# Attention projections of a hybrid decoder block: q and k of four heads moved together, v first

## The chip, the cores and the metric

The kernel runs on one core of one Trainium2 chip. The metric is the time of one execution on the device, in microseconds (us); the time of a kernel is the median of its runs.

## The reference

One decoder layer on 1024 tokens of width 1024. The part that matters here is branch A, attention in three groups of eight heads of width 64, each group with its own window and dilation:

```python
h = rms_norm(x, norm_mix)
proj = h @ w_in                                  # 1024 x 1024 by 1024 x 10768
qkv_a, ... = split_columns(proj, IN_WIDTHS)      # 3 x 1536 columns: q, k, v
qkv_a = qkv_a.reshape(b, s, 3, 3, 8, 64)         # (q,k,v) x group x head x width
qa = rms_norm(qkv_a[:, :, 0], q_norm)            # over the 64 of a head
ka = rms_norm(qkv_a[:, :, 1], k_norm)
for gi, (win, dil) in enumerate(((128, 1), (512, 4), (2048, 16))):
    o_g, lse_g = dilated_window_attention(qa[:, :, gi], ka[:, :, gi], va[:, :, gi], win, dil)
o_a = sum(softmax(lse over the groups) * o_g)
...
```

Behind it stand a gated DeltaNet branch, gates, an output projection, a mixture of 16 experts and a last gated addition. The change does not touch them.

## The kernel before

All matmuls of the projections are made in three passes over split operands: each fp32 operand is written as a rounded part and a rest, and `mm3` (L36) issues rounded x rounded, rounded x rest and rest x rounded. `norm_h` (L128) normalises x and leaves its transpose split in `k.hh` and `k.hl` (eight blocks c of 128 channels by 1024 tokens). Weights come in pieces of 512 KB: `wraw` (L169) issues the transfer on SP's queue into one of two raw buffers, and `wsplit` (L177) makes the two parts, the rounded one on ScalarE (L182), the rest on VectorE (L183), in one of three pairs of buffers.

The attention stage (`attention`, L1310) has six units u of four heads: `hh, g = divmod(u, 3)` gives half and group. `attn_stream` (L355) projects one unit: first q, then k, then v, each in eight token tiles t of 128, each tile 24 matmuls (8 blocks, 3 passes) with the hidden state stationary and 256 weight columns moving, and yields once per tile: 24 pieces of 24 matmuls. ScalarE copies each result out of PSUM (L403) and, for q and k, squares it (L406); VectorE sums the squares per head (L407). After four tiles `norm` (L366) takes the inverse root (`rsqrt_ln`, L114: logarithm and exponential on ScalarE, small operations on VectorE), multiplies (L369) and queues two turns, each of which transposes four token tiles on PE (L374) into the one buffer of the PSUM pool `ps_t` and copies them to `qT` or `kT` on ScalarE with the gain (L378); the list `late` hands out one turn per piece. v of the groups 1 and 2 is regrouped through DRAM (`regroup`, L345). The weights of the next third are loaded at t = 5 (L417).

`attn_heads` (L425) is the softmax of a unit in ten steps: step i transposes the weights of token tile i-1 (`turn`, L465), multiplies those of tile i-2 with v (`value`, L475), and makes the scores of tile i (`score`, L447), which VectorE masks while it takes the maximum (L450, L452) and ScalarE exponentiates (L454). A tile sees 256 keys in group 0 (but for its first tile) and in every other tile of group 1, else 128.

The loop of `attention` (L1332) advances the softmax of unit u while it iterates over the projection of unit u+1, by the rule of L1343: step n comes with piece i when `10 * (i + 1) // 24` reaches it, so a step every 2 or 3 pieces. Beside unit 3 run `group_weights` and `combine_groups` (L508, L562), which combine the three groups of the first half; their scale-and-add is on VectorE (L582, L584), with broadcast transfers on SP's queue (L596). The last unit runs beside gate jobs (`channels`, L201, 512 moving columns), four yields per group, ten steps over 40 yields. Between unit 0's projection and the first softmax stand the decay tables (`dn_tables`, L223). A scheduler orders each engine's instructions from this program; it keeps near to the program's order.

Of the kernel before, what the change touches and what calls it, by code (L numbers as in the profile page):

```python
# [7 lines left out]
F32 = mybir.dt.float32  # L8
# [3 lines left out]
AF = mybir.ActivationFunctionType  # L12
ALU = mybir.AluOpType
AX = mybir.AxisListType
# [5 lines left out]
T = 8  # L20
C = 8
# [106 lines left out]
def norm_h(k):  # L128

    nc = k.nc  # L130
# [4 lines left out]
    v = k.I["norm_mix"]  # L135
    xs = []
    for t in range(T):
        if t % 2 == 0:
            xx = k.at.tile([128, 2, 1024], F32, name="x", tag="kT" if t < 4 else "vtok", bufs=2)
        x = xx[:, t % 2, :]  # L140
        for i in range(2 if t < 2 else 1):
            hs = slice(512 * i, 512 * i + 512) if t < 2 else slice(None)
            (nc.scalar if t < 2 and not i else nc.sync).dma_start(x[:, hs], k.I["x"][0, t * 128:t * 128 + 128, hs])
        if t == 0:
            nc.scalar.dma_start(g, bass.AP(tensor=v.tensor, offset=v.offset, ap=[[0, 128], [1, 1024]]))
        if t == 1:
            raw = attn_weights(k, 0, 0, 0, wraw)
        xs.append(x)
    for t in range(T):
        x = xs[t]  # L150
# [5 lines left out]
        if t == 0:  # L156
            with k.tc.issue_after(d.ins), k.tc.issue_after(k.last_exp.ins):
                ws = [wsplit(k, r) for r in raw]
# [64 lines left out]
def dn_tables(k):  # L223
# [9 lines left out]
    bc = k.at.tile([128, 1024], F32, name="bac", tag="qT", bufs=2)[0:32]  # L233
# [96 lines left out]
def attn_weights(k, g, hh, j, load=wload):  # L330
    w = k.I["w_in"][0].rearrange("(s c p) n -> s p c n", p=128, s=2)
    o = 1536 * j + 512 * g + 256 * hh
    return [load(k, [(slice(None), w[s][:, :, o:o + 256])], shape=(4, 256)) for s in range(2)]
# [21 lines left out]
def attn_stream(k, u, out, ws=None):  # L355
# [5 lines left out]
    ws = ws or attn_weights(k, g, hh, 0)  # L361
    late = []
# [3 lines left out]
    def norm(j, hf, raw, ss, dst):  # L366
        v = raw.rearrange("p t (h d) -> p (t h) d", d=64)
        rs = rsqrt_ln(k, at, ss[:, 4 * hf:4 * hf + 4, :].rearrange("p a b -> p (a b)"), 64.0)
        nc.vector.tensor_tensor(v, v, rs[:, :, None].to_broadcast([128, 16, 64]), op=ALU.mult)  # L369

        def turn(pr):
# [6 lines left out]
            nc.scalar.activation(turned_view(dst[:, pr, :], g, hf), src, AF.Copy, scale=k.gq if j == 0 else k.gk)  # L378
        late.extend([None, lambda: turn(0), lambda: turn(1)])

    for j in range(3):
        if j == 2:
            v = at.tile([128, T, 256], F32, name="vtok", bufs=2)
            out.append(v)
        if j == 2 and g == 0:
            rows = [v[:, t, :] for t in range(T)]
        elif j == 2:
            raw = [at.tile([128, 4, 256], F32, name="qraw", bufs=3) for _ in range(2)]
            rows = [raw[t // 4][:, t % 4, :] for t in range(T)]
        else:  # L390
            raw = [at.tile([128, 4, 256], F32, name="qraw", bufs=3) for _ in range(2)]
            rows = [raw[t // 4][:, t % 4, :] for t in range(T)]
            ss = at.tile([128, T, 4], F32, name="ss", bufs=2)
            dst = at.tile([128, 2, 1024], F32, name="qT" if j == 0 else "kT", bufs=2)
            out.append(dst)
        nxt = None
        for t in range(T):
            p = k.ps_mm.tile([128, 256], F32, name="mm", tag="mm")
            for c in range(C):
                hi, lo = ws[c // 4]  # L400
                s = slice(t * 128, t * 128 + 128)
                mm3(nc, p, k.hh[:, c, s], k.hl[:, c, s], hi[:, c % 4, :], lo[:, c % 4, :], c == 0, c == C - 1)
            nc.scalar.activation(rows[t], p, AF.Copy)  # L403
            if j < 2:
                sq = at.tile([128, 4, 64], F32, name="sqa", bufs=2)
                nc.scalar.activation(sq.rearrange("p a b -> p (a b)"), p, AF.Square)  # L406
                nc.vector.tensor_reduce(ss[:, t, :], sq, axis=AX.X, op=ALU.add)  # L407
            if late:
                f = late.pop(0)
                if f:  # L410
                    f()
            if j < 2 and t % 4 == 3:
                norm(j, t // 4, raw[t // 4], ss, dst)
            if j == 2 and g and t % 4 == 3:
                regroup(k, g, t // 4, raw[t // 4], v)
            if j < 2 and t == 5:
                nxt = attn_weights(k, g, hh, j + 1)  # L417
            yield
        ws = nxt
    for f in late:  # L420
        if f:
            f()
# [887 lines left out]
def attention(k):  # L1310
    tc, nc = k.tc, k.nc
    with ExitStack() as e:
# [6 lines left out]
        k.at = e.enter_context(tc.tile_pool(name="at", bufs=1, reuse_waits="tile"))  # L1319
        setup(k)  # L1320
# [11 lines left out]
        for u in range(6):  # L1332
            heads = attn_heads(k, u, *st)
# [6 lines left out]
            for i, _ in enumerate(attn_stream(k, u + 1, st) if u < 5 else more):  # L1340
# [541 lines left out]
```

## Time and profile before

| | |
|---|---|
| median of 3 runs | 2051.33 us (2045.94 to 2053.91) |
| the profiled execution, its own time | 2063.92 us |
| its span | 2062.2 us |
| PE busy | 1962.6 us, 95% |
| VectorE, ScalarE busy | 1161.1 us, 968.1 us |
| moved by DMA | 252.53 MB, mean 122 GB/s |

The profiled execution takes 12.6 us more than the median of the runs. The attention stage ends at about 592 us of the span. Matmuls are pipelined: the time from one start to the next is their cost, the durations overlap.

### The profile page before, as it was taken

How to read it: one execution, taken by the hardware profiler on the slowest of the kernel's cores; microseconds unless marked ns; L12 is line 12 of the kernel's file. 1: busy time of each engine (PE TensorE's matmuls, PEld its weight loads, DVE VectorE, ACT ScalarE, POOL GpSimd, SP SyncE). 2: the span in 40 equal slices, each digit the busy share in tenths (PEclk: the TensorE clock that was granted, in tenths of full speed). 3: DMA queues.
4: the chain of work that ended last, by engine and by line, in shares of the span. 5: the costliest groups of instructions: out<-in, count | busy, mean ns of one | idle time of the engine just before them, and what ended most of it. 6: DMA issues, size and time to landing. Idle time of an engine off the chain costs nothing.

```text
span 2062.2 us, 35105 instructions
## 1 busy us (share of the span) xinstructions
PE 1962.6 (95%) x13402; PEld 1672.1 (81%) x13402; DVE 1161.1 (56%) x2940; ACT 968.1 (47%) x2573; POOL 195.4 (9%) x196
## 2 busy tenths in 40 slices
PE   7999999999999989999999999979999889999998
PEld 7999999989987777777777777858978767777698
DVE  7253435473422678778877872355474645555655
ACT  6344445444443644565456452232433345555643
POOL 0000000000000001010000100000021244431100
PEclk9999999999999999999999999989999899999999
DMA  4102131242233222232222223585465377776742
GB/s 160 54 28 78 53 105 52 81 138 74 66 110 111 58 67 59 65 85 62 79 76 74 68 68 101 145 246 192 145 204 184 125 238 253 231 246 229 244 157 91
DMA packets 249353, 252.53 MB, mean 122 GB/s; under 512 B 62453, under 2 KB 207142, under 8 KB 248922
## 3 DMA queue, kind: packets, MB, share of 16 engines
q1 hardware_dynamic: 234280, 224.88, 35.8%
q0 software_dynamic: 11776, 24.18, 3.4%
q8 instruction: 107, 1.75, 0.3%
q10 hardware_dynamic: 3122, 1.16, 0.2%
q14 instruction: 68, 0.56, 0.1%
HBM read 202.34 MB, written 64.59 MB: 129 GB/s over the span
## 4 chain that ended last, share of the span: by engine, by line
PE 63%; DVE 14%; DMA 12%; issue 7%; ACT 2%; POOL 1%; SPq 1%; ACTq 0%; DVEq 0%; POOLq 0%
PE mm L37 13%; PE mm L38 13%; PE mm L39 12%; DMA M<-dA 4%; DVE prod L764 3%; DVE tu L766 3%; DMA wraw<-in_w_expert_down_dram 2%; PE gp L37 2%; DVE acc L636 2%; PE gp L39 2%; PE gp L38 1%; PE sc L447 1%; PE pv L475 1%; PE gu L37 1%; PE gu L38 1%
## 5 line engine op out<-in xcount | busy, mean ns | idle before, releaser
L183 DVE TENSOR_TENSOR wlo<-wraw,whi 128x1024 fp32r<-128x1024 f32 x228 | 274.9, 1223 | 213.2 <-ACT whi L182 211.3
L37 PE MATMUL mm<-whi,hTh 128*128 128x256 f32 x1152 | 336.1, 292 | 5.9 <-ACT sqa L406 3.5
L37 PE MATMUL mm<-hTh,whi 128*128 128x512 f32 x768 | 327.0, 426 | 14.7 <-ACT th L962 10.3
L38 PE MATMUL mm<-wlo,hTh 128*128 128x256 f32 x1152 | 327.8, 285 | 0.0
L39 PE MATMUL mm<-whi,hTl 128*128 128x256 f32 x1152 | 327.7, 284 | 0.0
L182 ACT ACTIVATE whi<-wraw 128x1024 fp32r<-128x1024 f32 x228 | 236.0, 1057 | 194.2 <-PE mm L38 113.9
L39 PE MATMUL mm<-hTh,wlo 128*128 128x512 f32 x768 | 304.8, 397 | 0.0
L38 PE MATMUL mm<-hTl,whi 128*128 128x512 f32 x768 | 303.8, 396 | 0.0
L37 PEld LDWEIGHTS mm<-whi,hTh 128*128 128x128 f32 x1152 | 221.8, 193 | 18.0 <-issue 7.3
L38 PEld LDWEIGHTS mm<-wlo,hTh 128*128 128x128 f32 x1152 | 222.1, 193 | 0.8 <-DVE wlo L183 0.7
L39 PEld LDWEIGHTS mm<-whi,hTl 128*128 128x128 f32 x1152 | 221.8, 193 | 0.2 <-DVE rsqx L119 0.2
L37 PEld LDWEIGHTS mm<-hTh,whi 128*128 128x128 f32 x768 | 146.3, 191 | 40.8 <-ACT th L962 10.7
L39 PEld LDWEIGHTS mm<-hTh,wlo 128*128 128x128 f32 x768 | 145.2, 189 | 32.9
L38 PEld LDWEIGHTS mm<-hTl,whi 128*128 128x128 f32 x768 | 146.4, 191 | 22.4
L454 ACT ACTIVATE sm<-sm,nm 128x128 f32<-128x128 f32 (+1 forms) x192 | 84.3, 440 | 87.5 <-DVE nm L452 87.0
L403 ACT ACTIVATE qraw<-mm 128x256 f32<-128x256 f32 x128 | 48.4, 378 | 148.2 <-PE mm L39 148.0
L407 DVE TENSOR_REDUCE ss<-sqa 128x4 f32<-128x256 f32 x96 | 40.1, 418 | 133.0 <-ACT sqa L406 132.9
L636 DVE SCALAR_TENSOR_TENSOR acc<-xp,cols,acc 128x512 f32<-128x512 f32 x144 | 107.7, 748 | 8.1 <-ACT acc L634 5.1
L466 DVE COPY pT<-pt 128x256 f32<-128x256 f32 (+1 forms) x96 | 49.4, 540 | 105.0 <-PE pt L465 105.0
L764 DVE TENSOR_TENSOR prod<-tu,M 128x2 f32<-128x2 f32 (+30 forms) x248 | 83.7, 337 | 6.2
L1520 PE MATMUL gr<-wraw,hr 128*64 128x256 f32 x512 | 67.0, 381 | 9.7 <-ACT hr L1511 9.6
L37 PE MATMUL mm<-whi,mh 128*128 128x256 f32 x256 | 73.6, 289 | 0.1
(402 smaller groups left out, 4077.5 us busy)
## 6 DMA issues: line engine op xcount, KB each, us to landing
wraw<-in_w_in_dram SPq DMA_DIRECT2D x84, 512.0 KB
wraw<-in_w_expert_down_dram SPq DMA_DIRECT2D x30, 512.0 KB
wraw<-in_w_expert_gate_dram SPq DMA_DIRECT2D x60, 256.0 KB
wraw<-in_w_expert_up_dram SPq DMA_DIRECT2D x60, 256.0 KB
gT<-th SPq DMA_DIRECT2D x32, 256.0 KB
wraw<-in_w_branch_b_dram SPq DMA_DIRECT2D x16, 512.0 KB
gate<-gT SPq DMA_DIRECT2D x32, 256.0 KB
wraw<-in_w_out_dram SPq DMA_DIRECT2D x16, 512.0 KB
```

Source lines behind the costliest of these rows:

```text
L37: nc.tensor.matmul(out, lh, rh, start=start, stop=False)
L38: nc.tensor.matmul(out, lh, rl, start=False, stop=False)
L39: nc.tensor.matmul(out, ll, rh, start=False, stop=stop)
L182: nc.scalar.activation(hi, raw, AF.Copy)
L183: nc.vector.tensor_tensor(lo, raw, r32(hi), op=ALU.subtract)
L403: nc.scalar.activation(rows[t], p, AF.Copy)
L454: nc.scalar.activation(x.sm[:, h, :nk], x.sm[:, h, :nk], AF.Exp, bias=nm[:, h:h + 1], accum_out=ml[:, x.t, h, 1:2])
L466: nc.vector.tensor_copy(x.pT[:, 2 * pr:2 * pr + 2, :nk], pt[:, :, :nk])
L636: nc.vector.scalar_tensor_tensor(acc, xp[:, i:i + 512], k.conv(i, b), acc, op0=ALU.mult, op1=ALU.add)
L764: nc.vector.tensor_tensor(pr[:, :j, :n], tu[:, :j, :n], M[:, None, :n, r].to_broadcast([128, j, n]), op=ALU.mult)
L766: nc.vector.tensor_reduce(tu[:, :j, r], pr[:, :j, :n], axis=AX.X, op=ALU.add)
L1520: k.nc.tensor.matmul(self.p[64 * f:64 * f + 64], self.t[:, c, :], w[:, f], start=c == 0, stop=c == 7)
```

## The change

v is projected first, in eight tiles of 256 columns. q and k follow together, in eight tiles of 512 columns: a weight piece now holds two blocks c with 256 columns of q beside 256 of k (`attn_raw`, two transfers per piece), and there are four such pieces and two for v. `attn_next` takes the six pieces of every unit in one sequence: it splits the next raw piece and starts the transfer of the one after the following; a fourth pair of split buffers (`k.wx`) serves three pieces of every two units. The eight-tile q-k half yields twice per tile, after 12 and after 24 matmuls, so a unit still has 24 pieces. The normalisation works on q and k of four token tiles at once (32 head rows per token, 2048 elements). The turns of the first half of the tokens come in pairs in the middle of tiles 6 and 7, those of the second half (`pre`) in tiles 1 and 2 of the next unit's v. `qT` and `kT` have one buffer each and not two. The softmax steps start at piece 3 and end at piece 18: `(10 * (i - 2) + 16) // 17`.

```diff
-def attn_weights(k, g, hh, j, load=wload):
...
+def attn_raw(k, u, i):
+    hh, g = divmod(u, 3)
+    o = 512 * g + 256 * hh
+    if i < 2:
+        w = k.I["w_in"][0].rearrange("(s c p) n -> s p c n", p=128, s=2)
+        return wraw(k, [(slice(None), w[i][:, :, o + 3072:o + 3328])], shape=(4, 256))
+    w = k.I["w_in"][0].rearrange("(s c p) n -> s p c n", p=128, s=4)
+    return wraw(k, [((slice(None), slice(None), slice(256 * j, 256 * j + 256)),
+                     w[i - 2][:, :, o + 1536 * j:o + 1536 * j + 256]) for j in range(2)], shape=(2, 512))
+def attn_next(k):
+    u, i = divmod(k.an, 6)
+    own = k.wpool, k.wbufs
+    if (u % 2, i) in ((0, 1), (0, 5), (1, 3)):
+        k.wpool, k.wbufs = k.wx, (0, 1)
+    w = wsplit(k, k.ar.pop(0))
+    k.wpool, k.wbufs = own
+    k.an += 1
+    if k.an + 1 < 36:
+        k.ar.append(attn_raw(k, *divmod(k.an + 1, 6)))
+    return w
...
 def attn_stream(...):
-        late.extend([None, lambda: turn(0), lambda: turn(1)])
-    for j in range(3):
...
+        return [lambda pr=pr: turn(pr) for pr in (0, 2, 1, 3)]
+    v = at.tile([128, T, 256], F32, name="vtok", bufs=2)
+    for t in range(T):
...
+        nc.scalar.activation(raw[:, t % 4, :] if g else v[:, t, :], p, AF.Copy)
+        if t in (1, 2):
+            for f in pre[2 * t - 2:2 * t]:
+                f()
...
+        if t in (2, 4):
+            qk.append(attn_next(k))
+        if t == 7:
+            qk += [attn_next(k), attn_next(k)]
+        yield
...
+    for t in range(T):
...
+        if t == 6:
+            dst += [at.tile([128, 2, 1024], F32, name=n) for n in ("qT", "kT")]
+        p = k.ps_mm.tile([128, 512], F32, name="mm", tag="mm")
+        for c in range(C):
+            hi, lo = qk[c // 2]
+            mm3(nc, p, k.hh[:, c, s], k.hl[:, c, s], hi[:, c % 2, :], lo[:, c % 2, :], c == 0, c == C - 1)
+            if c == 3:
+                if t == 7 and u < 5:
+                    nxt.append(attn_next(k))
+                for f in late[:2] if t > 5 else ():
+                    f()
+                late = late[2:] if t > 5 else late
+                yield
...
+        if t == 7 and u < 5:
+            nxt.append(attn_next(k))
+        yield
...
 def attention(k):
-                while n < 10 * (i + 1) // (24 if u < 5 else 40):
+                while n < ((10 * (i - 2) + 16) // 17 if u < 5 else 10 * (i - 1) // 38):
```

How the order moves, at two places (the numbers are those of buffers). ScalarE beside the second unit's projection, from the exponentials (`sm,ml<-sm,nm`) of the first unit's tile 3 to those of its tile 4. Before:

```order
L454 ACTIVATE sm_1776,ml_1411<-sm_1776,nm_1777 128x256 x4
L403 ACTIVATE qraw_1682<-mm_1791 128x256
L406 ACTIVATE sqa_1817<-mm_1791 128x256
L378 ACTIVATE qT_1323<-qkT_1820,gq_391 128x4x128
L403 ACTIVATE qraw_1682<-mm_1826 128x256
L406 ACTIVATE sqa_1852<-mm_1826 128x256
L478 ACTIVATE ot_1664<-pv_1878 128x2x128
L120 ACTIVATE rsqy_1856<-rsqx_1855 128x16
L121 ACTIVATE rsqy_1856<-rsqy_1856 128x16
L454 ACTIVATE sm_1891,ml_1411<-sm_1891,nm_1892 128x256 x4
```

Now:

```order
L485 ACTIVATE sm_1443,ml_1194<-sm_1443,nm_1444 128x256 x4
L444 ACTIVATE qraw_1402<-mm_1404 128x512
L446 ACTIVATE sqa_1471<-mm_1404 128x512
L509 ACTIVATE ot_1344<-pv_1487 128x2x128
L485 ACTIVATE sm_1500,ml_1194<-sm_1500,nm_1501 128x256 x4
```

Before, the results of two projection tiles (`qraw` and `sqa` from two `mm`) stood between the two steps; now one stands there, of which half the matmuls lie ahead of the first step.

VectorE at the end of a half of four projection tiles, from the last sum of squares (`ss<-sqa`) to the product (`qraw<-qraw,rsqy`). Before:

```order
L407 TENSOR_REDUCE ss_1322<-sqa_1456 128x4
L119 TENSOR_SCALAR rsqx_1459<-ss_1322 128x16
L122 TENSOR_TENSOR rsqz_1461<-rsqy_1460 128x16
L123 SCALAR_TENSOR_TENSOR rsqz_1461<-rsqz_1461,rsqx_1459 128x16
L124 SCALAR_TENSOR_TENSOR rsqy_1460<-rsqz_1461,rsqy_1460 128x16
L369 TENSOR_TENSOR qraw_1320<-qraw_1320,rsqy_1460 128x1024
```

Now, at the end of the second unit's projection:

```order
L447 TENSOR_REDUCE ss_1736<-sqa_1918 128x8
L119 TENSOR_SCALAR rsqx_1921<-ss_1736 128x32
L183 TENSOR_TENSOR wlo_2044<-wraw_1890,whi_2043 128x1024
L122 TENSOR_TENSOR rsqz_1923<-rsqy_1922 128x32
L183 TENSOR_TENSOR wlo_2124<-wraw_1935,whi_2123 128x1024
L123 SCALAR_TENSOR_TENSOR rsqz_1923<-rsqz_1923,rsqx_1921 128x32
L124 SCALAR_TENSOR_TENSOR rsqy_1922<-rsqz_1923,rsqy_1922 128x32
L389 TENSOR_TENSOR qraw_1735<-qraw_1735,rsqy_1922 128x2048
```

Two weight splits (`wlo`) of the next unit's q and k now stand inside the normalisation, and the product is twice as wide.

On PE the order of the change has 12 matmuls of 512 columns between the softmax steps of pieces 8 and 9 and between those of pieces 13 and 14, and 24 of 256 columns between those of pieces 3 and 4; before, no two steps of the units 0 to 4 were closer than 48 of 256 columns. The first of the four turns of a unit's second half stands behind 61 matmuls of the next unit's v, the others follow after 7 matmuls each; in tiles 6 and 7 of q and k 4 and 6 matmuls of 512 columns separate the turns of a pair. Before, at least 24 matmuls stood between two turns.

## Rows read from the trace of the kernel before

**Rows 1.** The page: part 1 (busy time of each engine, its share of the span, instructions) and the first line of part 4 (the chain that ended last, share of the span by engine).

```profile
PE 1962.6 (95%) x13402; PEld 1672.1 (81%) x13402; DVE 1161.1 (56%) x2940; ACT 968.1 (47%) x2573; POOL 195.4 (9%) x196
...
PE 63%; DVE 14%; DMA 12%; issue 7%; ACT 2%; POOL 1%; SPq 1%; ACTq 0%; DVEq 0%; POOLq 0%
```

**Rows 2.** Busy time of each engine in three stretches of the attention stage (stretch and its length in us; busy us of PE, its weight loads, VectorE, ScalarE and GpSimd, with instruction counts; granted clock as a share of full speed; DMA share; GB/s).

```profile
110.00:390.00 280.00, 279.84 (x2453) 264.65 (x2452) 117.95 (x408) 128.95 (x409) 2.31 (x3) 1.00 0.22 64
390.00:440.00 50.00, 48.37 (x419) 44.91 (x417) 35.85 (x98) 21.92 (x73) 0.00 (x0) 1.00 0.52 149
440.00:592.00 152.00, 150.03 (x1258) 139.63 (x1259) 60.39 (x192) 67.08 (x205) 2.05 (x3) 0.98 0.29 83
```

**Rows 3.** Who waited for whom between 110 and 592 us (engine, tile and line that waited, what ended the wait: us in total, times, longest).

```profile
ACT qraw L403 <- PE mm L39: 128.3, 72, 4.5
...
PE mm L37 <- ACT sqa L406: 3.5, 1, 3.5
```

**Rows 4.** Timeline of PE in the middle of a projection group (start in us, duration, line, operation, output<-inputs, shapes). The start of one to the start of the next is what an instruction costs; durations overlap.

```profile
435.74 0.28 PE L37 MATMUL mm<-whi,hTh 128*128 128x256 f32 x1
...
437.78 0.28 PE L39 MATMUL mm<-whi,hTl 128*128 128x256 f32 x1
```

**Rows 5.** Timeline of PE in three stretches with 512 moving columns: gate jobs (the transposed hidden state moves; 21 matmuls from the first row to the second), an expert (the weights move; 17 matmuls) and the output projection (the weights are stationary; 12 matmuls).

```profile
594.44 0.39 PE L37 MATMUL mm<-hTh,whi 128*128 128x512 f32 x1
...
598.98 0.39 PE L39 MATMUL mm<-hTh,wlo 128*128 128x512 f32 x1
...
1662.86 0.39 PE L38 MATMUL gu<-wlo,hgh 128*128 128x512 f32 x1
...
1666.52 0.40 PE L39 MATMUL gu<-whi,hgl 128*128 128x512 f32 x1
...
1560.42 0.39 PE L37 MATMUL mm<-oah,whi 128*128 128x512 f32 x1
...
1562.99 0.40 PE L39 MATMUL mm<-oah,wlo 128*128 128x512 f32 x1
```

**Rows 6.** Timeline of one softmax step with 256 keys: the scores on PE, the first of four masks and the negated maximum on VectorE, then the exponentials of head 0, 2 and 3 on ScalarE; the row behind the last begins where that exponential's sum has been read.

```profile
142.80 1.13 PE L447 MATMUL sc<-kT,qT 64*128 64x256 f32 x8
...
143.96 0.42 DVE L450 CUSTOM_DVE_ANT_0 sm<-sc,m 128x256 f32<-128x256 f32 x1 [0.96 <-PE sc L447]
...
145.46 0.17 DVE L452 TENSOR_SCALAR nm<-ml 128x4 f32<-128x4 f32 x1
...
145.67 0.51 ACT L454 ACTIVATE sm<-sm,nm 128x256 f32<-128x256 f32 x1 [2.37 <-DVE nm L452]
...
146.67 0.49 ACT L454 ACTIVATE sm<-sm,nm 128x256 f32<-128x256 f32 x1
...
147.16 0.49 ACT L454 ACTIVATE sm<-sm,nm 128x256 f32<-128x256 f32 x1
...
147.65 0.36 ACT L403 ACTIVATE qraw<-mm 128x256 f32<-128x256 f32 x1
```

**Rows 7.** Timeline of PE where the matmul stream is broken: four transposes of q or k, then eight of the weights, then the scores, then the first two matmuls of the next group.

```profile
521.92 0.60 PE L374 MATMUL qkT<-ident,qraw 128*128 128x128 f32 x4
522.36 0.60 PE L465 MATMUL pt<-ident,sm 128*128 128x128 f32 x4
...
523.91 1.13 PE L447 MATMUL sc<-kT,qT 64*128 64x256 f32 x8
524.98 0.38 PE L37 MATMUL mm<-whi,hTh 128*128 128x256 f32 x1
525.20 0.28 PE L38 MATMUL mm<-wlo,hTh 128*128 128x256 f32 x1
```

**Rows 8.** Timeline of one softmax step with 128 keys: the scores, the next matmul on PE, the last exponential and the reading of its sum.

```profile
330.80 0.71 PE L447 MATMUL sc<-kT,qT 64*128 64x128 f32 x8
...
331.45 0.39 PE L37 MATMUL mm<-whi,hTh 128*128 128x256 f32 x1
...
333.89 0.39 ACT L454 ACTIVATE sm<-sm,nm 128x128 f32<-128x128 f32 x1
...
334.19 0.19 ACT L454 ACTIVATION_READ_ACCUMULATOR sm<-sm,nm 128x1 f32 x1
```

**Rows 9.** Timeline of a softmax step that VectorE delayed: the scores, a weight split and a normalising product that stand between the masks, and the last exponential with the copy behind it.

```profile
133.45 1.14 PE L447 MATMUL sc<-kT,qT 64*128 64x256 f32 x8
...
134.59 1.22 DVE L183 TENSOR_TENSOR wlo<-wraw,whi 128x1024 fp32r<-128x1024 f32 x1
...
136.59 1.22 DVE L369 TENSOR_TENSOR qraw<-qraw,rsqy 128x1024 f32<-128x1024 f32 x1
...
140.23 0.49 ACT L454 ACTIVATE sm<-sm,nm 128x256 f32<-128x256 f32 x1
...
140.72 0.36 ACT L403 ACTIVATE qraw<-mm 128x256 f32<-128x256 f32 x1
```

**Rows 10.** Groups of instructions between 110 and 592 us (line, engine, operation, names, shapes, count | busy us, mean ns of one | idle before them, and what ended it).

```profile
L183 DVE TENSOR_TENSOR wlo<-wraw,whi 128x1024 fp32r<-128x1024 f32 x30 | 36.7, 1225 | 43.0 <-ACT whi L182 43.0
...
L407 DVE TENSOR_REDUCE ss<-sqa 128x4 f32<-128x256 f32 x79 | 33.1, 419 | 117.5 <-ACT sqa L406 117.3
...
L182 ACT ACTIVATE whi<-wraw 128x1024 fp32r<-128x1024 f32 x30 | 31.6, 1054 | 8.4 <-PE mm L39 8.4
...
L369 DVE TENSOR_TENSOR qraw<-qraw,rsqy 128x1024 f32<-128x1024 f32 x20 | 24.5, 1223 | 0.3
...
L378 ACT ACTIVATE qT<-qkT,gq 128x512 f32<-128x512 f32 x20 | 13.6, 682 | 0.0
```

**Rows 11.** Timeline of VectorE from a mean square (L119) to the product with its inverse root (L369).

```profile
434.53 0.17 DVE L119 TENSOR_SCALAR rsqx<-ss 128x16 f32<-128x16 f32 x1
...
435.98 1.23 DVE L369 TENSOR_TENSOR qraw<-qraw,rsqy 128x1024 f32<-128x1024 f32 x1
```

**Rows 12.** Timeline of VectorE in the unit that combines the groups: a scale that waited for its broadcast (in brackets the idle time before it and what ended it).

```profile
431.79 1.17 DVE L582 TENSOR_TENSOR fb<-fb,og 128x512 f32<-128x512 f32 x1 [2.40 <-DMA fb<-fT]
```

More of the change, by code (lines that the diff above doesn't have):

```diff
@@ L146, in norm_h @@
         if t == 1:
-            raw = attn_weights(k, 0, 0, 0, wraw)
+            k.an, k.ar = 0, [attn_raw(k, 0, i) for i in range(2)]
         xs.append(x)
@@ L157, in norm_h @@
             with k.tc.issue_after(d.ins), k.tc.issue_after(k.last_exp.ins):
-                ws = [wsplit(k, r) for r in raw]
+                ws = [attn_next(k) for _ in range(2)]
         for j in range(2):
@@ new lines, in attn_stream @@
+    dst = []
+    late = []
+    nxt = []
+    for t in range(T):
+        if t % 4 == 0:
+            raw = at.tile([128, 4, 512], F32, name="qraw", bufs=2)
+            ss = at.tile([128, 4, 8], F32, name="ss", bufs=2)
+        if t == 6:
+            dst += [at.tile([128, 2, 1024], F32, name=n) for n in ("qT", "kT")]
+        p = k.ps_mm.tile([128, 512], F32, name="mm", tag="mm")
+        s = slice(t * 128, t * 128 + 128)
+        for c in range(C):
+            hi, lo = qk[c // 2]
[4 more added lines that the diff above has]
+                for f in late[:2] if t > 5 else ():
+                    f()
+                late = late[2:] if t > 5 else late
+                yield
+        nc.scalar.activation(raw[:, t % 4, :], p, AF.Copy)
+        sq = at.tile([128, 8, 64], F32, name="sqa", bufs=2)
+        nc.scalar.activation(sq.rearrange("p a b -> p (a b)"), p, AF.Square)
+        nc.vector.tensor_reduce(ss[:, t % 4, :], sq, axis=AX.X, op=ALU.add)
+        if t % 4 == 3:
+            late += norm(t // 4, raw, ss, dst)
+        if t == 7 and u < 5:
+            nxt.append(attn_next(k))
+        yield
@@ L425, in attn_heads @@
+    out += [*dst, v, nxt, late]
 def attn_heads(k, u, qT, kT, v):
@@ L1339, in attention @@
             first = chain(group_weights(k, 0), combine_groups(k, 0)) if u == 3 else None
-            for i, _ in enumerate(attn_stream(k, u + 1, st) if u < 5 else more):
+            for i, _ in enumerate(attn_stream(k, u + 1, st, ws, pre) if u < 5 else more):
+                if u == 5 and i == 1:
+                    for f in pre:
+                        f()
                 if first:
                     next(first, None)
-                while n < 10 * (i + 1) // (24 if u < 5 else 40):
+                while n < ((10 * (i - 2) + 16) // 17 if u < 5 else 10 * (i - 1) // 38):
                     next(heads, None)
```

74 lines of the change are left out of this document (21 added, 53 removed).

## The prediction

> **What bounds the kernel now.** I read the page first: TensorE is busy for 95% of the span and the chain that ended last lies on PE for 63% of it, VectorE and ScalarE come to about half [rows 1]. That is an average over stages, so I read the stretches of the attention stage, the only part that the diff touches. From 110 to 390 us PE is busy for 279.8 of 280 us, at the full granted clock (1.00, the 2.4 GHz level), while VectorE and ScalarE have more than half of their time free [rows 2]. The waits of 110 to 592 us say the same: ScalarE waits 128.3 us for projection matmuls, and PE waits for anything only once, 3.5 us, for a ScalarE square [rows 3]. So in this stage the time is the sum of PE's instructions. A change gains what it takes out of that sum, and loses every wait it opens, since no slack on PE absorbs one.
>
> **What a projection matmul costs.** Moving 256 columns, 17 steps from 435.74 to 437.78 us make 120 ns each [rows 4]. Moving 512, 20 steps of the gate jobs make 4.54 us, 227 ns; 16 of the experts, where the weights move as they will here, make 3.66 us, 229 ns; 11 of the output projection make 2.57 us, 234 ns [rows 5]. So 512 columns cost less than 2 x 120 = 240 ns: the difference of 107 ns is the extra 256 columns, and some 13 ns is paid per instruction, whatever its width.
>
> The Trainium skill, "TensorE: Matmul & The Clock Gate", section "Back-to-back issue gap", gives N/2.4 + 2.5 ns for a warm matmul. By it 256 columns cost 109 and 512 cost 216 ns, and merging two would give 2.5 ns instead of some 12. The rows disagree with it for both widths, so I take the rows.
>
> **The change, part by part.**
>
> *Merged matmuls.* Per head unit, q and k took 384 matmuls of 256 columns and now take 192 of 512; six units make 1152 merges. Each gives 240 - 227 = 13 ns at best and 240 - 234 = 6 ns at worst. I take 228, nearest to the rows where the weights move and to those right behind the attention stage: 12 ns x 1152 = **-13.8 us**, between -7.4 and -15.0. It is all on the path.
>
> *Short gaps between score and transpose.* Ten steps of the softmax of the unit before are woven into 24 pieces. They now start at piece 3 and end at piece 18, so three gaps per unit hold one piece and not two: one of 24 matmuls of 256 columns (2.88 us), two of 12 of 512 (2.74 us). Before, the gap was 5.76 us, and PE did not wait for it. With 256 keys the scores hold PE for 1.07 us [rows 7], and the last exponential ends 147.65 - 142.80 = 4.85 us after they start [rows 6]. PE arrives at 1.07 + 2.74 = 3.81 and needs the last head after six transposes of 0.11 us [rows 7], at 4.47: 0.4 us of wait. With 128 keys PE arrives at 0.65 + 2.74 = 3.39 and the last exponential is done at 334.28 - 330.80 = 3.48 [rows 8], before its transposes come up at 3.7: none. Of 15 short gaps six have 256 keys, two of them in the unit that also combines the groups (below). Four x 0.4 = **+1.6 us**. These are the chains when VectorE is free. A late one, held by a weight split and a normalising product, ended 140.72 - 133.45 = 7.27 us after the scores started [rows 9], so the upper end is 2.4 us more in each of 15 gaps, some 36 us. I take the free chain, because in the new order the products of q and k stand behind the last score and the splits are done about when the scores begin.
>
> *Normalising q and k together.* The product now covers 2048 elements: two of 1.22 [rows 10], 2.45 us. That of the second half of the tokens is followed on PE by the transposes, which stand 61 matmuls into the next unit's v: cover 61 x 0.12 = 7.3 us. In that time come the copy and square of the last group (two reads of 512 columns, 0.68 each [rows 10]), the reduction (twice 0.42 less its fixed part, about 0.7 [rows 10]), the 1.45 us from mean square to product [rows 11], two weight splits that the order puts in between (1.22 each [rows 10]) and the product: 1.4 + 0.7 + 1.45 + 2.45 + 2.45 = 8.4 us if nothing overlaps. ScalarE's half of a split does overlap the logarithm and exponential, so I take 8.0: PE waits 0.7 us at each of four unit boundaries, **+2.8 us** (0 to 6). At the first boundary the decay tables stand in between, and at the last the gate jobs do: **+1 us** for the two.
>
> *Turns in pairs.* The transposed q and k go through one PSUM buffer, and the second of a pair now follows after 7 matmuls of 256 columns: 0.44 + 0.84 = 1.28 us after the first begins. The first takes 0.60 on PE [rows 7] and 0.68 on ScalarE [rows 10], with a handover: 0.1 us, three times at four boundaries, **+1.2 us**. The pairs inside the q-k groups have 0.91 us or more and wait for nothing worth counting.
>
> *Breaks in the matmul stream.* Of 16 breaks per unit there were two where a turn and a softmax step shared one; now there are 18. The second matmul after a break comes 0.22 and not 0.12 us after the first [rows 7]: 2 x 5 x 0.1 = **+1 us**.
>
> *The unit that combines the groups* (390 to 440 us). VectorE runs its scale-and-add beside the softmax; one of its waits for a broadcast took 2.40 us [rows 12], and the one wait of PE in the stage, 3.5 us [rows 3], lies here. The new order spreads the softmax differently, so that wait can go. But its two short gaps cost 0.4 and, where a scale stands ahead of the masks, some 1.2, and a late broadcast up to 2.4 more. I take **0**, from -2 to +4.
>
> *Costed at nothing.* The copies, squares and sums of 512 columns are half as many; ScalarE and VectorE had slack, which hid them. Weight bytes are the same; each q-k piece is two transfers instead of one, hidden because a piece is fetched about a piece before its split, and the fourth split buffer lets both of the next unit's v pieces be split before q-k ends. If that cover went, v's first matmuls would wait for a split of 1.05 + 1.22 us [rows 10]. One buffer for qT and kT is written six pieces behind the last score that reads it.
>
> **Sum.** -13.8 + 1.6 + 2.8 + 1 + 1.2 + 1 + 0 = -6.2 us. Of the profiled execution's 2063.9 us this leaves 2057.7. The median of the runs shown is 12.6 us lower than that execution; the saving is the same there: 2051.3 - 6.2 = **2045 us**. A measurement of this kernel tells about 0.5% (10.3 us) from no change.
>
> **The rivals.**
>
> *The waits stay hidden.* For it: PE arrives late by less than 1 us in every wait priced above, and one more overlap closes each. Against it: no slack on PE. Then 12 to 15 us remain: 2037 to 2039 us, faster by more than the bound. Chance 0.30.
>
> *The short gaps run late* (slower). Place: the transposes of the three early steps per unit, behind the exponentials. If each is held as in rows 9, six gaps cost 0.4 + 2.4 and nine 5.9 - 3.7 = 2.2: 36.6 us, with the 6 us of the other terms and -13.8 some +29: 2080 us. It eats the gain from (13.8 - 6) / 15 = 0.5 us per gap, and reaches the bound on the slower side from 1.2 us. For it: chains of that length stand in the trace. Against it: what delayed them there has been moved away from the scores. Chance 0.11 for slower than the bound.
>
> *The saving is not per instruction.* If merging gave only 2.5 ns, 1152 merges would give 2.9 us, and with 7.6 us of waits the time would be 2056 us, within the bound. Against it: 227 ns at 512 columns [rows 5]. This is the page's rule named above; by it and by no row the gain vanishes. Chance 0.06.
>
> That the program would not do what the diff says is ruled out: the order of PE shows the matmuls of 512 columns and the gaps as counted.
>
> **How the numbers follow.** The forecast, saving kept and 4 to 14 us of waits, has 0.53; about 0.06 of it lies beyond the bound on the faster side. Faster 0.30 + 0.06 = 0.36; same 0.47 + 0.06 = 0.53; slower 0.11. The range reaches from the whole of the largest saving (2051 - 15, less 1 for the spread of a median) to the smallest with the waits as priced and the combining unit late (2051 - 7.4 + 7.6 + 4, and some 5 for late gaps): 2035 to 2060.
>
> **What would show it.** On the page: 384 rather than 1152 matmuls of 256 columns on each of the three lines, and 227 to 229 ns between those of 512. In the waits of the attention stage: transposes of the weights waiting for exponentials, 0.4 us each; transposes of q and k waiting for the product, under 1 us, four times. The stage's end moves from 592 to about 586 us, and the stages behind it keep their length. Wrong would be: a spacing near 234 (the saving is halved), waits of a microsecond or more in most short gaps (slower), or PE waiting for split weights at the start of v.

## The result, and the profile after

The changed kernel took **2065.05 us** (median of 6 runs, 2060.3 to 2068.4) beside 2052.03 for the kernel before (6 runs, 2045.9 to 2058.0): ratio 1.0059, 95% interval [1.0035, 1.0082], some 12 us slower where 6 us faster was forecast, and just outside the range of 2035 to 2060.

The profiled executions do not show this at first sight: after has a span of 2058.7 us, before one of 2062.2. The profiled execution of before was slower than every timed run of its kernel, that of after about as fast as the fastest of its own. So whole spans must not be compared here, and the stages must be read one by one. The last transposes of the second heads' group weights, which close the attention stage (its last unit runs beside the gate jobs, hence later than the 592 us of the prediction), move from 664.2 to 674.0 us: **the changed stage is 9.8 us longer**. The code behind it is the same, and what it takes differs between two executions by more than that.

The page of after, part 1 and the first line of part 4 (answers to [rows 1]):

```profile
PE 1963.8 (95%) x12250; PEld 1606.8 (78%) x12250; DVE 1154.3 (56%) x2832; ACT 962.0 (47%) x2453; POOL 194.5 (9%) x196
...
PE 48%; DVE 13%; DMA 11%; issue 4%; ACT 3%; SPq 1%; POOL 1%; DVEq 0%; ACTq 0%; POOLq 0%
```

The 1152 instructions less are there (13402 to 12250), and PE's busy time is no shorter. The same three stretches as [rows 2], and two of 12 us:

```profile
110.00:390.00 280.00, 278.46 (x1868) 232.14 (x1866) 115.50 (x366) 125.56 (x350) 2.31 (x3) 1.00 0.21 62
390.00:440.00 50.00, 46.94 (x338) 37.78 (x339) 27.63 (x73) 20.76 (x62) 1.50 (x2) 1.00 0.58 176
440.00:592.00 152.00, 148.42 (x914) 119.28 (x913) 63.94 (x172) 63.72 (x167) 0.55 (x1) 0.97 0.23 68
...
444.00:456.00 12.00, 9.13 (x60) 6.85 (x58) 7.90 (x20) 4.43 (x15) 0.00 (x0) 0.96 0.36 111
456.00:468.00 12.00, 12.00 (x48) 7.56 (x48) 3.02 (x11) 4.71 (x17) 0.00 (x0) 0.62 0.14 40
```

PE now idles in each of them, and from 456 to 468 us it is "busy" all the time at a granted clock of 0.62, most of it at the lower level, 1.2 GHz. There busy time is not work done. The waits of PE between 110 and 592 us, where before had one [rows 3]:

```profile
PEld pt L496 <- ACT sm L485: 8.1, 13, 3.1
...
PE pt L496 <- ACT sm L485: 4.3, 3, 2.9
...
PE qkT L394 <- DVE qraw L389: 3.4, 4, 1.4
```

Transposes of the weights wait for exponentials, and turns of q and k for the normalising product, as forecast, but longer. The merged matmuls stand on PE as follows (19 steps from the first row to the second; compare [rows 4] and [rows 5]):

```profile
243.91 0.40 PE L39 MATMUL mm<-whi,hTl 128*128 128x512 f32 x1
...
248.26 0.39 PE L37 MATMUL mm<-whi,hTh 128*128 128x512 f32 x1
```

4.35 us in 19 steps are 229 ns each, the foreseen spacing. So the spacing is right and the time is wrong.

To find the loss I compared the units: from the first scores of a unit to those of the next, PE does nearly the same work in every kernel here (softmax of one unit, projections of the next). Two units differ. Unit 0 of the rows that begin with "after" holds 12 more transposes of q and k (1.5 us), which elsewhere stand ahead of its first scores. Unit 4 of the three kernels with later turns, and of "before, even steps", holds one piece of 24 matmuls (2.9 us) less, because its first scores come a piece later. Times in us; the last column is where the last transposes of the second group weights start. The kernels below the first two are those of the experiments.

```
kernel                       unit 0  unit 1  unit 2  unit 3  unit 4   end
before                         97.0    93.2    88.2   103.6    90.0   664.2
after                         100.1    93.9    89.2   109.7    89.7   674.0
after, even steps              99.0    93.0    89.3   106.9    88.5   668.3
  and turns later              95.6    91.7    88.6   101.8    85.9   660.4
  and combining on GpSimd      95.6    91.7    88.3    96.9    85.9   654.7
  turns later, in halves       97.2    93.4    90.2   103.0    87.7   669.6
after, combining on GpSimd    100.1    94.0    89.2   102.2    89.7   667.5
after, no combining           101.0    94.1    88.0    98.4    91.2   664.2
before, no combining           97.0    93.2    87.7    97.0    90.0   657.6
before, even steps             96.8    92.9    88.7   101.4    86.9   661.7
```

Unit 3, which combines the groups, loses 6.1 us, unit 0 3.1 (half of it the transposes just named), and the others, where the merge alone should have given 2 us each, gain next to nothing.

**A short gap.** Timeline of PE in after, where a step stands one piece behind the last:

```profile
240.17 0.39 PE L39 MATMUL mm<-whi,hTl 128*128 128x512 f32 x1
240.40 1.06 PE L496 MATMUL pt<-ident,sm 128*128 128x128 f32 x6
241.39 0.43 PE L506 MATMUL pv<-pT,vtok 128*64 128x128 f32 x2
241.75 0.44 PE L496 MATMUL pt<-ident,sm 128*128 128x128 f32 x2
242.12 0.65 PE L506 MATMUL pv<-pT,vtok 128*64 128x128 f32 x6
242.70 0.71 PE L478 MATMUL sc<-kT,qT 64*128 64x128 f32 x8
```

From 240.40 to 242.70 are 2.30 us. An undisturbed step with as many transposes and products of values takes 1.56 (226.98 to 228.53 us of the same trace). Only 0.26 us of the 0.74 are a visible wait, of the weight load of the last two of the six transposes:

```profile
241.02 0.20 PEld L496 LDWEIGHTS pt<-ident,sm 128*128 128x128 f32 x2 [0.26 <-ACT sm L485]
```

The rest falls where the transposes and the products of values, normally eight of each in a row, alternate and stand further apart. That the late exponentials cause this order is read from the rows; experiment 2 shows that it goes with the short gap.

**A turn.** VectorE at a unit's end in after, then PE:

```profile
203.28 0.18 DVE L119 TENSOR_SCALAR rsqx<-ss 128x32 f32<-128x32 f32 x1
203.51 1.23 DVE L183 TENSOR_TENSOR wlo<-wraw,whi 128x1024 fp32r<-128x1024 f32 x1
204.65 0.18 DVE L122 TENSOR_TENSOR rsqz<-rsqy 128x32 f32<-128x32 f32 x1
205.40 1.22 DVE L183 TENSOR_TENSOR wlo<-wraw,whi 128x1024 fp32r<-128x1024 f32 x1 [0.56 <-ACT whi L182]
206.54 0.18 DVE L123 SCALAR_TENSOR_TENSOR rsqz<-rsqz,rsqx 128x32 f32<-128x32 f32 x1
...
206.99 2.29 DVE L389 TENSOR_TENSOR qraw<-qraw,rsqy 128x2048 f32<-128x2048 f32 x1
...
208.38 0.28 PE L37 MATMUL mm<-whi,hTh 128*128 128x256 f32 x1
209.43 0.63 PE L394 MATMUL qkT<-ident,qraw 128*128 128x128 f32 x4 [0.77 <-DVE qraw L389]
```

Both weight splits stand inside the chain from mean square to product, the second with a wait of its own, so L119 to L389 takes 3.71 us, where [rows 11] has 1.45. PE starts the turn 1.05 us behind a matmul of 0.12, a loss of 0.93; at the other three boundaries 0.78, 1.53 and 0.82.

**Unit 3.** The last step before 456 us in after:

```profile
448.38 1.13 PE L478 MATMUL sc<-kT,qT 64*128 64x256 f32 x8
...
448.78 0.69 DVE L615 TENSOR_TENSOR acc<-acc,fb 128x512 f32<-128x512 f32 x1
...
451.80 1.14 DVE L613 TENSOR_TENSOR fb<-fb,og 128x512 f32<-128x512 f32 x1 [0.54 <-DMA fb<-fT]
...
452.86 0.40 DVE L481 CUSTOM_DVE_ANT_0 sm<-sc,m 128x256 f32<-128x256 f32 x1
...
454.23 0.68 DVE L615 TENSOR_TENSOR acc<-acc,fb 128x512 f32<-128x512 f32 x1
454.84 0.15 DVE L483 TENSOR_SCALAR nm<-ml 128x4 f32<-128x4 f32 x1
...
455.73 0.69 PE L496 MATMUL pt<-ident,sm 128*128 128x128 f32 x2 [2.87 <-ACT sm L485]
...
463.74 0.63 PE L39 MATMUL mm<-whi,hTl 128*128 128x512 f32 x1
464.16 0.63 PE L37 MATMUL mm<-whi,hTh 128*128 128x512 f32 x1
```

The scores end at 449.5, but VectorE reaches their masks at 452.86, behind a sum, copies, a reduction and a scale that waited for its broadcast; a second sum stands between the masks and the negated maximum (L483) that the exponentials need. Behind the end of the scores 1.8 us of this are work of the combining (the scale and the second sum) and 0.54 its waiting. PE, one piece later, waits 2.87 us, and then runs at half speed: 0.42 us from one 512-column matmul to the next at 463.74.

### The profile page after: what moved, and what is told of

Same layout as the page of the kernel before. It is cut to its first block, busy times and chain, and to the rows that moved or that the text cites. A ratio compares the mean times of both kernels' runs of the same rounds, so it can differ in the third digit from the quotient of the medians.

```text
span 2058.7 us, 32660 instructions
## 1 busy us (share of the span) xinstructions
PE 1963.8 (95%) x12250; PEld 1606.8 (78%) x12250; DVE 1154.3 (56%) x2832; ACT 962.0 (47%) x2453; POOL 194.5 (9%) x196
## 4 chain that ended last, share of the span: by engine, by line
PE 48%; DVE 13%; DMA 11%; issue 4%; ACT 3%; SPq 1%; POOL 1%; DVEq 0%; ACTq 0%; POOLq 0%
PE mm L37 9%; PE mm L39 9%; PE mm L38 9%; DMA M<-dA 4%; DVE prod L795 3%; DVE tu L797 3%; DMA wraw<-in_w_expert_down_dram 2%; PE gp L37 2%; DVE acc L667 2%; PE gp L39 2%; PE gp L38 1%; PE gu L38 1%; PE gu L37 1%; PE gu L39 1%; PE yp L1573 1%
## 5 line engine op out<-in xcount | busy, mean ns | idle before, releaser
L37 PE MATMUL mm<-whi,hTh 128*128 128x256 f32 (+1 forms) x768 | 267.9, 349 | 2.3 <-ACT hTh L1022 2.3
L38 PE MATMUL mm<-wlo,hTh 128*128 128x256 f32 (+1 forms) x768 | 261.8, 341 | 0.0
L39 PE MATMUL mm<-whi,hTl 128*128 128x256 f32 (+1 forms) x768 | 261.1, 340 | 0.0
L37 PEld LDWEIGHTS mm<-whi,hTh 128*128 128x128 f32 x768 | 146.2, 190 | 28.7 <-issue 9.3
L39 PEld LDWEIGHTS mm<-whi,hTl 128*128 128x128 f32 x768 | 146.0, 190 | 16.2 <-DVE rsqx L119 0.2
L38 PEld LDWEIGHTS mm<-wlo,hTh 128*128 128x128 f32 x768 | 146.3, 190 | 13.9
L447 DVE TENSOR_REDUCE ss<-sqa 128x8 f32<-128x512 f32 x48 | 32.9, 685 | 123.3 <-ACT sqa L446 122.5
L481 DVE CUSTOM_DVE_ANT_0 sm<-sc,m 128x128 f32<-128x128 f32 (+1 forms) x192 | 56.1, 348 | 64.3 <-PE sc L478 53.3
```

The source lines that it names most:

```text
L37: nc.tensor.matmul(out, lh, rh, start=start, stop=False)
L38: nc.tensor.matmul(out, lh, rl, start=False, stop=False)
L39: nc.tensor.matmul(out, ll, rh, start=False, stop=stop)
L481: nc.vector.tensor_tensor_reduce(x.sm[:, h, :nk], sc[h % 2][:, h // 2, :nk], mask, 1.0, -3.0e38, op0=ALU.add, op1=ALU.max, accum_out=ml[:, ...
```

## The experiments

Each ratio is to the kernel before, run beside it on the same chip; the changed kernel itself is 1.0059 [1.0035, 1.0082].

**1. Slow the combining**, in the changed kernel and in the kernel before.

```
-            first = chain(group_weights(k, 0), combine_groups(k, 0)) if u == 3 else None
+            if u == 3:
+                first = chain(group_weights(k, 0), combine_groups(k, 0))
...
-                if first:
+                if first and i % 2:
...
-            for _ in first or ():
+            for _ in first or () if u == 4 else ():
```

> The changed kernel, but the combining of the first four heads takes a step at every second piece of units 3 and 4, where it took one at every piece of unit 3. Theory 1 (the combining unit is where the time went: its scale-and-adds wait on VectorE for broadcasts and hold up the softmax's masks behind them): in the trace of the changed kernel unit 3 takes 109.45 us from its first scores to those of unit 4, and unit 0, which has the same softmax steps and no combining, 100.10. So 9.35 us go, from 2065 to about 2056, and the wait of 3.0 us on TensorE at 452.6 us and the 9 us at the lower clock behind it are gone. Rival (the short distances between softmax steps are to blame, combining or not): unit 3 keeps its waits of 1 us and more, and the time stays over 2062.

> The kernel before with the same edit as the first run: a control. Its unit 3 takes 103.42 us and its unit 0 97.01. Theory 1: 6.4 us go, from 2052 to about 2045.6, so that the distance between the two kernels shrinks from 13 us to about 10, because the combining costs the changed kernel 3 us more than the kernel before. Rival (the wait of 3.6 us in unit 3 of the kernel before has nothing to do with the combining's pace): no more than 2 us go.

Measured: 1.0035 [1.0022, 1.0047] and 1.0002 [0.9987, 1.0018]. Unit 3 took 108.6 us in the changed kernel and 105.1 in the control, against 109.7 and 103.6. By the timing the changed kernel gains 5 us of the 9.4 expected (the intervals allow none), by the stage's end 1.5 (674.0 to 672.5), by unit 3 itself 1.1; the control gains nothing of its 6.4. A miss: PE's wait of 2.9 us is still there, from 452.3 us on. At half its pace the combining costs the changed kernel about the same; whether the combining is the cause was left open.

**2. Even steps**, in the changed kernel and, as a control, in the kernel before (where the same rule for u < 5 takes the place of its own).

```
-                while n < ((10 * (i - 2) + 16) // 17 if u < 5 else 10 * (i - 1) // 38):
+                while n < (min(10, (i - 1) // 2) if u < 5 else 10 * (i - 1) // 38):
```

> The changed kernel with its ten softmax steps at pieces 3, 5, 7 and so on to 21: two pieces of the stream between any two, where it has one piece in three or four places of each unit. Theory 2 (a step one piece behind the last finds its exponentials late, and its transposes and products of values then wait on each other): outside unit 3 the transposes and products of values took 4.0 us more than before (1.45, 1.23, 0.0 and 1.27 us in units 0, 1, 2 and 4), and these go; in unit 3, where the same intervals grew by 8.4 us, about half goes, since its steps still meet the combining: about 2057. Rival (theory 1 alone, the combining): the 4.0 us are no more than the order of the same work, and 2063 or more is left.

> The kernel before with softmax steps at pieces 3, 5, 7 and so on to 21, as a control of the even steps, which took 11 us off the changed kernel. Theory 2 (only a step one piece behind the last costs, and the kernel before has none: its steps are two or three pieces apart): no more than 2 us either way, 0.999 to 1.001. Rival (even steps help any such kernel): 3 us or more are gained, and the gain was not the change's own loss.

Measured: 1.0003 [0.9989, 1.0016], and the control 0.9997 [0.9985, 1.0009]. The changed kernel gains some 11 us by the timing (6 to 17 by the intervals) and 5.7 by the stage's end, 2.8 of them in unit 3. The transposes and products of values of unit 1 take 12.4 us again, as before; in after they took 13.7. The kernel before, which had no short gaps, gains nothing that the timing can tell. Its stage does end 2.5 us earlier, but 2.2 of these are in unit 3, where a wait of 1.1 us stands in place of the 3.5; its units 0 to 2 move by 0.5 us or less. So outside unit 3 the gain is that of the short gaps, and theory 2 holds there; in unit 3 even steps help both kernels.

**3. The merge undone**, first in the changed kernel, then in the one of experiment 4 with its waits out of the way.

```
-            mm3(nc, p, k.hh[:, c, s], k.hl[:, c, s], hi[:, c % 2, :], lo[:, c % 2, :], c == 0, c == C - 1)
+            for n in (slice(0, 256), slice(256, 512)):
+                mm3(nc, p[:, n], k.hh[:, c, s], k.hl[:, c, s], hi[:, c % 2, n], lo[:, c % 2, n], c == 0 and not n.start, c == C - 1 and n.start > 0)
```

> The changed kernel with each matmul of 512 columns of q and k issued as two of 256, in the same place and order otherwise. Theory 3 (the merge itself saves what the spacing in the traces says, 230 against two times 120 ns, 1152 merges): 11.5 us are lost, to about 2076.5. Rival (the merge saves nothing by itself, as the matmuls start in the time that their columns take): 2065, and spacing near 115 ns in the halves.

> The changed kernel with even steps and later turns, each matmul of 512 columns of q and k issued as two of 256. Theory 3 (the merge saves 10 ns each by the spacing, 230 against two times 120, over 1152 merges): 11.5 us are lost, from 0.9973 to about 1.003 of the kernel before. Rival (as the forecast had it: 12 ns each, 13.8 us): 1.004. Rival (spacing saved comes back as waits, since the softmax is as late as before): 0.9985 or less.

Measured: 1.0097 [1.0074, 1.0120] and 1.0052 [1.0033, 1.0072]. The first pair (1.0097 against 1.0059) says 8 us, with intervals that allow 1 to 15; its stage ends 12.6 us later (686.6 against 674.0), but its trace also has stretches at the lower clock at 308 and 414 us that after's has not. The second pair (1.0052 against 0.9973) says 16 us, with intervals that allow 11 to 21; its stage ends 9.2 us later (669.6 against 660.4), 1.2 to 1.8 us in each unit. The halves start 120 ns apart (median), as before the change. The merge does save time, 8 ns each by the second pair's stage; the timing and the first pair do not agree closely enough to say it better.

**4. Turns a piece later**, on top of even steps (here at pieces 4 to 22), and then also the combining between the steps.

```
-        if t in (1, 2):
-            for f in pre[2 * t - 2:2 * t]:
+        if t in (2, 3):
+            for f in pre[2 * t - 4:2 * t - 2]:
...
+                while n < (min(10, (i - 2) // 2) if u < 5 else 10 * (i - 1) // 38):
```

> The changed kernel with two edits: softmax steps at pieces 4, 6 and so on to 22, two pieces apart, and the last four turns of q and k at the third and fourth blocks of the next v where they stood at the second and third. Theory (the turns wait for the normalising product): TensorE's waits of 0.93, 0.78, 1.53 and 0.82 us before these turns are gone, so 4 us less than the run with even steps alone, which stood at 1.0003 of the kernel before: about 0.998 of it. Rival (the wait only moves: the first scores of a unit now stand close behind the copies of the turned blocks): no more than 1 us is gained.

> The kernel of the run before this one, with the combining's steps on every second piece of units 3 and 4, always the piece between two softmax steps. Theory 1 (the combining's scale-and-adds wait for broadcasts ahead of the softmax's masks on VectorE): behind the masks they hold up nothing for a piece, so unit 3, which took 106.9 us with even steps alone, comes down to about 100, near unit 0's 99.0: 7 us less than the run before this one, about 0.995 of the kernel before. Rival (what makes unit 3 late is not the scale's place but the traffic and SyncE's queue: slowing the combining alone took only 1.1 us off unit 3): unit 3 stays at 105 us or more.

Measured: 0.9973 [0.9962, 0.9985] and 0.9976 [0.9965, 0.9986]. The first beats both kernels. PE's waits for the product, 3.4 us in the row above, are down to this row of its trace:

```profile
PE qkT L394 <- DVE qraw L389: 0.4, 1, 0.4
```

From even steps alone the gain is 6 us by the timing and 7.9 by the stage, more than the 4.1 us of the four waits; what the step's shift by a piece adds was not separated. The second edit gave nothing: unit 3 took 103.1 us where the first run had 101.8, with a wait of 2.7 us from 454.0 on. Where the program puts the scale does not decide. The rival was right on that, though not on its 105 us.

**5. No combining**, in both kernels (a generator that only stores zeros in its place).

```
-            first = chain(group_weights(k, 0), combine_groups(k, 0)) if u == 3 else None
+            first = combine_none(k, 0) if u == 3 else None
```

> The changed kernel without the combining of the first four heads in unit 3: its weights, broadcasts, products and sums are left out, and zeros are stored in its place. Theory 1: unit 3 takes unit 0's 100.1 us where it took 109.5, 9.4 us less: 1.0013 of the kernel before. Compared with the next run it prices the rest of the change alone. Rival (unit 3 is slow for another reason, as the even g = 0 steps behind the copies through memory for unit 4's v): it keeps 105 us or more.

> The kernel before with the same left out. Theory 1: unit 3 takes 97.0 us where it took 103.4, so 0.997 of the kernel before. The distance to the run before this one is then what the change costs with no combining: 9 us if the unit of the combining explains only 3 of the 12, as the unit lengths say (3.09 us longer in unit 0, 0.94 and 0.82 in units 1 and 2). Rival (the combining explains the whole loss): the two stand within 3 us.

Measured: 1.0003 [0.9990, 1.0016] and 0.9973 [0.9958, 0.9988]. Without the combining the change costs 6 us and not 12, by the stage's end 6.6 and not 9.8; by unit 3's length the combining costs 11.3 us after (109.7 - 98.4) and 6.6 before (103.6 - 97.0). Neither of the two theories alone carries the loss: a third to a half is the combining meeting the new steps, and the rest stands without it. Most of that rest is in unit 0, 4.0 us, with the 12 transposes in it and, in this run, a longer wait for the product than in after.

**6. The combining on GpSimd**, in the changed kernel and in that of experiment 4.

```
-        nc.vector.tensor_tensor(half_view(acc if g == 0 else f, g), half_view(f, g), group_shape(x, g), op=ALU.mult)
+        nc.gpsimd.tensor_tensor(half_view(acc if g == 0 else f, g), half_view(f, g), group_shape(x, g), op=ALU.mult)
...
-            nc.vector.tensor_tensor(acc, acc, f, op=ALU.add)
+            nc.gpsimd.tensor_tensor(acc, acc, f, op=ALU.add)
```

> The changed kernel with the combining's products and sums in unit 3 on GpSimd, where they were on VectorE; broadcasts, pace and order stay. Theory 1, in its sharper form (VectorE takes its work in order, so a scale that waits for a broadcast holds the masks and the copies behind it; the traffic itself does no harm): the waits of 1 to 3 us and the stretch at the lower clock behind them go, unit 3 falls from 109.5 us to near the 98.4 it took with no combining at all, so the run stands near the 1.0003 of that one. Rival (the transfers of the combining, of v through memory and of weights hold each other up): unit 3 keeps 106 us or more, and the run stands over 1.004.

> The changed kernel with even steps and later turns (0.9973 of the kernel before) and the same move to GpSimd. If what is left in unit 3 is VectorE's wait alone, unit 3 falls from 101.8 us to unit 0's 95.6: 6 us less, about 0.994. Rival (GpSimd's own work, or the transfers): unit 3 keeps 100 us or more, and the time is no better than 0.997.

Measured: 1.0015 [1.0003, 1.0027] and 0.9953 [0.9936, 0.9970], 2047.1 against 2056.6 us: the fastest kernel here. The same work by groups between 396 and 510 us, on VectorE in after (columns as in [rows 10]):

```profile
L613 DVE TENSOR_TENSOR fb<-fb,og 128x512 f32<-128x512 f32 x8 | 9.0, 1125 | 8.3 <-DMA fb<-fT 7.9 <-issue 0.3
L615 DVE TENSOR_TENSOR acc<-acc,fb 128x512 f32<-128x512 f32 x8 | 5.5, 685 | 0.1
L613 DVE TENSOR_TENSOR acc<-fb,og 128x512 f32<-128x512 f32 x4 | 2.8, 692 | 3.8 <-DMA oaT<-acc 3.8
```

and on GpSimd in the first run of this experiment:

```profile
L613 POOL TENSOR_TENSOR fb<-fb,og 128x512 f32<-128x512 f32 x8 | 13.4, 1680 | 8.9 <-DMA fb<-fT 8.9
L615 POOL TENSOR_TENSOR acc<-acc,fb 128x512 f32<-128x512 f32 x8 | 10.3, 1290 | 0.6
L613 POOL TENSOR_TENSOR acc<-fb,og 128x512 f32<-128x512 f32 x4 | 6.2, 1555 | 13.0 <-DMA oaT<-acc 12.1 <-DMA fb<-fT 0.9
```

GpSimd is slower at each operation and idles longer ahead of them, 22 us against 12, and yet unit 3 falls from 109.7 to 102.2 us (from 101.8 to 96.9 with even steps and later turns), with the clock back (the stretches of the unit's end, columns as in [rows 2]):

```profile
444.00:456.00 12.00, 11.17 (x77) 8.08 (x77) 6.04 (x14) 4.33 (x15) 6.95 (x6) 1.00 0.55 168
456.00:468.00 12.00, 12.00 (x77) 9.51 (x73) 6.59 (x18) 4.27 (x14) 2.73 (x2) 1.00 0.22 51
```

That is the sharp form of theory 1 for 7.5 of the 11.3 us: the combining harms because VectorE, in order, has the softmax's masks and copies behind it. The move takes two things off VectorE at once, 17.3 us of work and the waits for transfers, and no run parts them. 3.8 us remain over the run with no combining, with waits of 0.5 to 0.7 us at steps a piece apart; whether the transfers have a share in these was not tried. In the kernel of experiment 4 unit 3 comes to 96.9 us, close to the 95.6 that were expected. The move was not tried in the kernel before, where the combining costs 6.6 us too.

## Why the prediction was wrong, step by step

In us of the attention stage. The measured column is from after's trace against before's, outside unit 3 for the short gaps; the merge is from the second pair of experiment 3, the last term from unit 3 of the runs named.

```
step of the prediction           forecast   measured
merged matmuls                     -13.8     -9.2
short gaps                          +1.6     +4.0
product of q and k, four waits      +2.8     +4.1
first and last boundary             +1       +1.5
turns in pairs                      +1.2     +1.3
breaks                              +1       not separated
the unit that combines the groups    0       +6.2 (its short gaps 1.5; the combining 11.3 - 6.6 = 4.7)
sum                                 -6.2     +7.9; the stage's end says +9.8
```

- **The step that failed** is "The unit that combines the groups ... I take **0**, from -2 to +4": it came to +6.2, beyond its own upper end, and with the mis-sized merge (below) makes 10.8 of the 14.1 us between the two sums. Before's 3.5 us wait [rows 3] did go, as that step held possible. But five score steps of the unit now lie between the combining's first and last operation (407 to 455 us), where before had four (399 to 446 us), some a piece apart. In the step shown the combining's scale, sum and wait hold the exponentials back by 2.4 us. That is within the 1.2 and 2.4 us that the step named; but it set these against the old wait at even, and it left out what stands behind such a wait, here 9 us at half the clock (some 5 us). I also read the old wait as 3.5 us; without the combining the unit is 6.6 us shorter. Behind the wait before's clock fell too, to 0.85 and 0.86 in these stretches (columns as in [rows 2]):

```profile
432.00:444.00 12.00, 8.53 (x63) 8.24 (x62) 9.78 (x25) 4.32 (x16) 0.00 (x0) 0.85 0.39 112
444.00:456.00 12.00, 12.00 (x94) 11.10 (x93) 6.08 (x15) 5.02 (x15) 0.00 (x0) 0.86 0.13 45
```

  The wait had a second price, and I had not read the granted clock behind the one wait that I had.
- **Short gaps** were right in place and cause, and too small: 0.4 us of waiting in four gaps, where transposes and products of values took 1.45, 1.23 and 1.27 us more in units 0, 1 and 4. (Unit 3 took 1.5 us more even without the combining.) I had priced the late exponential, not the order that breaks up around it. The rival that named these gaps (2080 us) had the right sign at too high a price.
- **The merge** was mis-sized: 12 ns each were forecast, 13.8 us, and undoing it cost 9.2 us of the stage, 8 ns each. The spacing accounts for little of that: after's median between 512-column matmuls is 229 ns, where I took 228. In unit 1 the time from the start of each projection matmul to the next instruction's start sums to 70.2 us, before to 70.9; without the 0.78 us wait for the product and the 0.3 us of the pairs, which have rows of their own, that is 1.8 us less in a unit, where 2.3 were forecast. The rest was not found. The Trainium skill, "TensorE: Matmul & The Clock Gate", section "Back-to-back issue gap", has a formula for a single warm matmul by itself that would have given 2.5 ns for each merge, 2.9 us in all. The 8 ns decide against it, and that rival is out.
- **The product**: the chain was right in all its parts, and the waits came at 0.78 to 1.53 us where 0.7 was forecast, because the second split's rounded part on ScalarE waits for its own transfer inside the chain (0.32 us at 204.3, 0.92 at 386.3). The first boundary is the same thing: there the decay tables' matmul waits, 1.65 us from the last matmul to it.
- **Right**: instruction counts and spacing of the merge, the copies and reductions at nothing, one buffer for qT and kT, no wait of v's first matmuls for split weights.
- **Open**: about 2 us of the stage are in no step. The timing of after (12 us) and its stage (9.8 us) differ by less than the timing's interval.

With the waits out of the way the forecast's idea holds: with even steps and later turns the changed kernel stands at 0.9973 of before, 1.0052 with the merge undone, while even steps alone leave the kernel before at 0.9997. The further step to 0.9953, by the combining on GpSimd, is not the change's own: the kernel before might gain from it as well, and that was not run.

## What to carry to other kernels

Where one engine fills a stage, a saving on it is the easy term; price the schedule that comes with it by what each in-order engine holds ahead of the next needed result, not by the chain alone. Try work that waits for transfers on an engine with nothing urgent behind it, even if it is slower there; here it paid. And compare stages, not spans, when the difference is smaller than the scatter of single executions.

## What the runs showed of the hardware

- A 3 us wait of TensorE cost more than itself. In after, 2.87 us of idle time ahead of 455.73 us were followed by 9 us at 1.2 GHz (0.42 us per matmul of 512 columns, granted clock 0.62 from 456 to 468 us, so some 5 us lost). Before's wait of 3.5 us had 0.85 and 0.86 around and behind it, some 3.5 us. The second price was not fixed: in the slowed run of experiment 1 the same 2.87 us had a clock of 0.73 behind them, in the first run of experiment 4 a wait of 2.5 us had this (12 us, clock 0.86, some 1.7 us lost):

```profile
432.00:444.00 12.00, 11.95 (x78) 9.18 (x76) 8.80 (x20) 5.06 (x17) 0.00 (x0) 0.86 0.57 154
```

  Where the longest wait of the stage was 1.4 us (the combining on GpSimd, changed kernel) the clock stayed at 1.00 from 110 to 640 us.
- GpSimd did a product of 128x512 in 1.56 to 1.68 us and a sum in 1.29, VectorE in 0.69 to 1.13 and 0.69. The Trainium skill, "GPSIMD Engine Reference", section "3.1 Elementwise — side-by-side cycle accounting", keeps elementwise work on VectorE since GpSimd takes about twice as long (1.96 for a sum of 2048 columns). The rows agree on the price, 1.5 to 2.3 times, but not on the choice: the move gained 4 us on the best kernel by the timing (0.9973 to 0.9953, with intervals that allow none) and 5.7 by its stage (660.4 to 654.7).
